# Turning the backward keys of a gated recurrence on VectorE, with DRAM in place of the full transpose

## The chip, the cores and the metric

The kernel runs on one core of a Trainium2 chip. Its engines run side by side, each through its own list of instructions in order: TensorE (PE in the profile; its weight loads are PEld), VectorE (DVE), ScalarE (ACT), GpSimd (POOL) and SyncE (SP), which issues nearly all DMA transfers. Semaphores hold an instruction until what it needs is there. The metric is the device time of one launch in microseconds (us), the median of several runs.

## The reference

One encoder block over 1024 tokens of width 1024: layer norm, one wide projection (11776 columns), a dilated window attention, a bidirectional gated recurrence, two gates, an output projection and a feed-forward part. The change lies in the recurrence. It has 8 heads with 128 key and 128 value channels, and is computed in chunks, once forwards and once backwards over the tokens:

```python
k_inv = k * jnp.exp(-cum)                       # cum: running log of the forget gate in a chunk
u = jnp.einsum('bhnck,bhncv->bhnkv', k * jnp.exp(cum_last - cum), v)
def step(state, inp):
    d, uu = inp
    return d[..., None] * state + uu, state
_, s_start = lax.scan(step, init, (decay, u))   # the state that each chunk starts from
o_inter = jnp.einsum('bhnck,bhnkv->bhncv', q_dec, s_start)
```

The product `u` sums over the tokens of a chunk. On TensorE the summed index must lie on the 128 partitions, for the keys as for the values.

## The kernel before, in words

All work is in 32-bit floats; the large projections are done as three products of split halves (`mm3`, lines 277 to 279, wide products of 128 x 512). The first phase runs these projections as one long stream of products (`stream`, 12 wide products per slot), four tiles of 128 columns at a time. Between the slots side work is fed in: the recurrence of head h as soon as its tiles are there, attention when its own are. This side work is a generator, and a number that it yields says how many slots pass before its next piece. So the list of pieces, with their yields, is the plan; a scheduler then orders the instructions of each engine by its own estimate of times, and what is written is the order in which each engine runs.

`hgrn_side` (line 1303) is the plan of one head. `hgrn_dir` prepares a direction in four steps: scans of the gates on VectorE (line 1189), then keys (`st["ki", d]`) by multiplications on GpSimd (lines 1197 and 1211), reciprocals (line 1208) and decayed queries (lines 1213 and 1216) on VectorE. Keys lie with the channel on the partition and the tokens of 8 chunks of 128 along the row. `hgrn_keys` (line 1219) turns them: eight 128 x 128 transposes on TensorE into two PSUM banks (line 1225), and two copies on ScalarE into tiles `hkT` of 128 x 512, one of a ring of five (`half`, line 791). `hgrn_states` (line 1230) multiplies seven turned chunks with the values (line 1240; four chunks from the first `hkT`, three from the second) and runs the states together on ScalarE and VectorE (lines 1242 and 1245). `hgrn_scores` (line 1249) and `hgrn_out` follow. The first direction's keys are turned after two steps of both directions, the second direction's right behind the first direction's states, three slots ahead of its own.

Nearly all transfers are issued by SyncE in one queue: weights (`wa`, line 256), stores of evacuated projections (`evh`, lines 578, 598, 609 and 628) and the fetches of the side work. An entry that waits, for its data or for its buffer, holds all that is queued behind it. Rows that are stored turned (`store_rows`, line 594) already go out in four transfers of 32 partitions x 16 runs of 32 floats.

Of the kernel before, what the change touches and what calls it, by code (L numbers as in the profile page):

```python
# [10 lines left out]
F32 = mybir.dt.float32  # L11
# [11 lines left out]
HALF = 512  # L23
# [56 lines left out]
class Block:  # L80
    evac_ahead = 1000

    def __init__(self, ctx, tc, x, ln_in_g, ln_in_b, w_in, hgrn_lb, hgrn_norm_g, w_att_up, w_hgrn_up,
                 w_o, ln1_g, ln1_b, w_ffn_in, w_ffn_out, ln2_g, ln2_b, tabs, out, dbg=None):
        self.tc, self.nc, self.ctx = tc, tc.nc, ctx
        self.x = x[0]
        self.ln = {"in": (ln_in_g, ln_in_b), "1": (ln1_g[0], ln1_b[0]), "2": (ln2_g[0], ln2_b[0])}
        self.w_in, self.lbw, self.ng = w_in[0], hgrn_lb, hgrn_norm_g[0]
        self.wa, self.wr, self.wo = w_att_up[0], w_hgrn_up[0], w_o[0]
        self.wfi, self.wfo, self.tabs, self.out = w_ffn_in[0], w_ffn_out[0], tabs, out[0]  # L90
        self.dbg = dbg or {}
        nc = self.nc

        self.npj = 0
        self.issued = {}
        self.psum = ctx.enter_context(tc.tile_pool(name="psum", bufs=1, space=PSUM))
        self.cst = ctx.enter_context(tc.tile_pool(name="cst", bufs=1))
        self.tiny = ctx.enter_context(tc.tile_pool(name="tiny", bufs=1))
        self.spare = self.pad(self.cst, CST_PAD)
        self.wpool = self.pool("wp", "right")  # L100
        self.wp = self.wpool.__enter__()
        dram = ctx.enter_context(tc.tile_pool(name="dram", bufs=1, space=DRAM))

        def scratch(name, n):
            if name in self.dbg:
                return [self.dbg[name][i] for i in range(n)]
            return [dram.tile([128, 1024], F32, name=f"{name}{i}") for i in range(n)]

        self.att_d = scratch("att", 4)
        self.rec_d = scratch("rec", 8)  # L110
        self.tg_d = scratch("tg", 16)
        self.n1_d = scratch("n1", 8)
        self.ahs_d = scratch("ahs", 8)
        self.hg_d = [{n: dram.tile([128, T], F32, name=f"hg{h}{n}") for n in ("t0", "t1", "q")}
                     for h in range(8)]
        self.at_d = [{(k, g): dram.tile([128, T], F32, name=f"at{j}{k}{g}") for k in "qk" for g in range(3)}
                     for j in range(4)]
        for h in range(8):
            self.hg_d[h].update({n: dram.tile([T, 128], F32, name=f"hg{h}{n}") for n in "vg"})
        for j in range(4):  # L120
            self.at_d[j].update({("v", g): dram.tile([T, 128], F32, name=f"at{j}v{g}") for g in range(3)})
        self.w_d = [dram.tile([32, 128], F32, name=f"wd{j}") for j in range(4)]
        self.td = [dram.tile([128, 4, HALF], F32, name=f"td{i}") for i in range(3)]
        self.gd = {p: dram.tile([128, NF // 2, HALF], F32, name=f"gd{p}") for p in range(1, 8)}
        self.consts()
# [1104 lines left out]
    def hgrn_states(self, st, d, kT, vT):  # L1230


        nc, dec = self.nc, st["dec", d]
        S = self.slot(6 + d, "hS", (8, 128))
        cs = list(range(8)) if d == 0 else list(range(7, -1, -1))
        for b in range(2):
# [4 lines left out]
            for jj, c, after in part:  # L1241
                nc.scalar.activation(S[:, after, :], ps[:, jj, :], AF.Copy, scale=dec[:, 2, c:c + 1])
            for _, c, after in part:
                if c != cs[0]:
                    nc.vector.scalar_tensor_tensor(S[:, after, :], S[:, c, :], dec[:, 2, c:c + 1], S[:, after, :],
                                                   op0=OP.mult, op1=OP.add)
        return S

# [23 lines left out]

    def hgrn_out(self, h, st, b, am, vT, S, sg):

        nc = self.nc
        po = self.ps_sd().rearrange("p (k c) -> p k c", k=4)
        for jj in range(4):
            c = 4 * b + jj
            terms = [(am[:, jj, :], vT[:, c, :])]
            if c > 0:  # L1280
                terms.append((st["qd", 0][:, c, :], S[0][:, c, :]))
            if c < 7:
                terms.append((st["qd", 1][:, c, :], S[1][:, c, :]))
            for n, (l, r) in enumerate(terms):
                nc.tensor.matmul(po[:, jj, :], l, r, start=(n == 0), stop=(n == len(terms) - 1))
        ss = self.smt.tile([128, 4], F32, name="hss", tag="hss", bufs=2)
        sq, on = self.half3("hsq"), self.half3("hon")
        nc.scalar.activation(sq, po, AF.Square)
        nc.vector.tensor_reduce(ss, sq, AX.X, OP.add)
        nc.gpsimd.tensor_scalar(ss, ss, 1.0 / 128, RMS_EPS, op0=OP.mult, op1=OP.add)  # L1290
        nc.gpsimd.tensor_tensor(ss, ss, self.mhalf[:, 0:4], OP.pow)
        g = sg[:, 4 * b:4 * b + 4, :]
        for jj in range(4):
            nc.vector.scalar_tensor_tensor(on[:, jj, :], po[:, jj, :], ss[:, jj:jj + 1], g[:, jj, :],
                                           op0=OP.mult, op1=OP.mult)
        r = g.rearrange("p k c -> p (k c)")
        nc.vector.transpose(r.rearrange("p (b k j) -> p k b j", b=4, k=4), on.rearrange("p k (b j) -> p k b j", j=32))
        dst = self.rec_d[h].rearrange("(b i) (h a x) -> a h i b x", b=4, h=2, a=4)
        for a in range(4):
            s = slice(32 * a, 32 * a + 32)  # L1300
            nc.sync.dma_start(dst[a, b], r[s, :].rearrange("i (b x) -> i b x", b=4))

    def hgrn_side(self, h, st):
        nc = self.nc
        vT = self.fetch_rows(5, "hv", self.hg_d[h]["v"])
        st["fa"] = self.slot(6, "fa")
        steps = [self.hgrn_dir(h, d, st) for d in range(2)]
        for _ in range(2):
            for z in steps:
                next(z)  # L1310
                yield 1
        k0 = self.hgrn_keys(st, 0)
        for z in steps:
            next(z)
        yield 2
        next(steps[0])
        yield 1
        S = {0: self.hgrn_states(st, 0, k0, vT)}
        k1 = self.hgrn_keys(st, 1)
        yield 2  # L1320
        next(steps[1])
        sg = self.fetch_rows(8, "hg", self.hg_d[h]["g"])
        yield 1
        S[1] = self.hgrn_states(st, 1, k1, vT)
        yield 3
        am = [self.hgrn_scores(st, b) for b in range(2)]
        yield -3
        for b in range(2):
            self.hgrn_out(h, st, b, am[b], vT, S, sg)
# [742 lines left out]
```

## Time and profile before

| what | value |
|---|---|
| median of 3 runs | 2017.85 us (2013.26 to 2018.37) |
| the profiled execution | 2016.71 us, its span 2014.9 us |
| PE / DVE / ACT / POOL busy | 98% / 68% / 45% / 50% of the span |
| granted TensorE clock, mean | 0.997 |
| mean share of the 16 DMA engines on SyncE's queue | 47.9% |
| issues on SyncE's queue in all | 1104 |

Rows of a timeline read: start and length in us, engine, line, operation, output<-inputs, shapes, count, and in brackets the idle time before it and what ended it. Rows of grouped instructions read: count, busy time in us, mean ns of one, idle time before. Rows of one line's instructions give the shortest, median and longest duration in ns; for transfers SPq is the issue on SyncE, and the landing is counted from the start of the issue. Heads are numbered 0 to 7 in the order in which they run; their recurrence lies between 100 and 960 us of the span.

### The profile page before, as it was taken

The page shows a single profiled execution, that of the slowest core. Times are in us where ns is not written, and L with a number is a line of the kernel's source. Part 1 is how long each engine was busy: PE and PEld are TensorE (multiplying, and loading weights), DVE is VectorE, ACT ScalarE, POOL GpSimd, SP SyncE. Part 2 cuts the span into 40 slices and gives each one's busy share as a digit, 9 for nine tenths or more (in the row PEclk, how much of TensorE's full clock was granted, in tenths as well). Part 3 has the DMA queues.
Part 4 walks back from the last instruction along what each step waited for, and adds up shares of the span by engine and source line. Part 5 has one row for each costly group of instructions (what it writes and reads, how often), then busy time and mean ns, then how long its engine had stood idle before and what let it go on. Part 6 is the DMA issues. An engine that isn't in the chain of part 4 may idle for free. (4 is left out here: it accounts for less than half of the span.)

```text
span 2014.9 us, 30820 instructions
## 1 busy us (share of the span) xinstructions
PE 1980.5 (98%) x10718; PEld 1640.8 (81%) x10718; DVE 1364.5 (68%) x2217; ACT 907.1 (45%) x1822; POOL 1006.3 (50%) x874
## 2 busy tenths in 40 slices
PE   7999999999999999999999999999999999999998
PEld 6688888888888888888888888888788888888886
DVE  7877746885467855797443236558777776767788
ACT  6554455543654446444464443345333333344541
POOL 6466643666455654565546562244666665620000
PEclk9999999999999999999999999999999999999999
DMA  5445645546455464555546377534434443447533
GB/s 162 126 121 151 164 131 149 140 119 173 108 158 141 132 156 118 152 147 151 141 122 190 121 252 245 156 121 141 140 127 136 145 137 125 144 166 276 167 103 123
DMA packets 416125, 301.17 MB, mean 149 GB/s; under 512 B 133153, under 2 KB 359394, under 8 KB 415970
## 3 DMA queue, kind: packets, MB, share of 16 engines
q1 hardware_dynamic: 410624, 282.14, 47.9%
q10 hardware_dynamic: 5346, 17.08, 2.2%
q8 instruction: 84, 1.38, 0.3%
q14 instruction: 71, 0.58, 0.1%
HBM read 204.96 MB, written 94.18 MB: 148 GB/s over the span
## 5 line engine op out<-in xcount | busy, mean ns | idle before, releaser
L229 POOL TENSOR_TENSOR w_lo<-wa,w_hi 128x512 fp32r<-128x512 f32 x272 | 366.3, 1355 | 230.5 <-ACT w_hi L219 216.6
L219 ACT CAST w_hi<-wa 128x512 fp32r<-128x512 f32 x272 | 168.2, 620 | 263.7 <-PE pj L278 166.2
L229 POOL TENSOR_TENSOR w_lo<-wsum,w_hi 128x512 fp32r<-128x512 f32 x88 | 127.8, 1462 | 111.1 <-PE sd L279 60.7
L229 POOL TENSOR_TENSOR w_lo<-f_raw,w_hi 128x512 fp32r<-128x512 f32 x66 | 101.2, 1540 | 51.5 <-ACT w_hi L219 50.3
L215 POOL TENSOR_TENSOR mv<-mv,mhalf 128x1 f32<-128x1 f32 x16 | 12.6, 790 | 221.7 <-DVE mv L214 221.6
L219 ACT CAST w_hi<-wsum 128x512 fp32r<-128x512 f32 x88 | 54.6, 621 | 116.7 <-PE sd L278 108.8
L277 PE MATMUL pj<-xt1hi,w_hi 128*128 128x512 f32 x252 | 99.0, 393 | 0.7 <-DVE evh L589 0.7
L219 ACT CAST gwsum<-a_raw 128x512 fp32r<-128x512 f32 (+1 forms) x78 | 48.1, 617 | 112.2 <-PE pj L278 56.0
L278 PE MATMUL pj<-xt1lo,w_hi 128*128 128x512 f32 x252 | 98.5, 391 | 0.0
L279 PE MATMUL pj<-xt1hi,w_lo 128*128 128x512 f32 x252 | 98.2, 390 | 0.0
L607 DVE TENSOR_TENSOR evh<-wkeep,pj 128x512 f32<-128x512 f32 x45 | 30.8, 685 | 99.4 <-PE pj L279 58.1
L727 POOL TENSOR_TENSOR wa<-wa,wa 128x512 f32<-128x512 f32 x46 | 65.8, 1431 | 57.1 <-DVE wa L726 56.2
L229 POOL TENSOR_TENSOR w_lo<-ws,w_hi 128x512 fp32r<-128x512 f32 x46 | 62.9, 1374 | 56.3 <-ACT w_hi L219 45.8
L755 ACT COPY wkeep<-pj 128x512 f32<-128x512 f32 x136 | 79.4, 585 | 4.9 <-DVE evh L577 4.7
L277 PE MATMUL pj<-xt2hi,w_hi 128*128 128x512 f32 x192 | 77.2, 403 | 2.0 <-ACT w_hi L219 2.0
L279 PE MATMUL pj<-xt2hi,w_lo 128*128 128x512 f32 x192 | 76.3, 397 | 2.0 <-POOL w_lo L229 2.0
L229 DVE TENSOR_TENSOR gwkeep<-a_raw,gwsum 128x512 fp32r<-128x512 f32 (+1 forms) x78 | 53.1, 681 | 36.1 <-ACT gwsum L219 33.3
L278 PE MATMUL pj<-xt2lo,w_hi 128*128 128x512 f32 x192 | 76.1, 396 | 0.8 <-DVE xt2lo L409 0.7
L277 PE MATMUL pj<-xt4hi,w_hi 128*128 128x512 f32 x192 | 76.2, 397 | 0.0
L278 PE MATMUL pj<-xb11lo,w_hi 128*128 128x512 f32 x192 | 75.3, 393 | 0.0
L278 PE MATMUL pj<-xt4lo,w_hi 128*128 128x512 f32 x192 | 75.2, 392 | 0.0
L277 PE MATMUL pj<-xb11hi,w_hi 128*128 128x512 f32 x192 | 75.0, 393 | 0.1
(438 smaller groups left out, 6481.7 us busy)
## 6 DMA issues: line engine op xcount, KB each, us to landing
wa<-in_w_in_dram SPq DMA_DIRECT2D x184, 256.0 KB, 3.4
f_raw<-in_w_ffn_in_dram SPq DMA_DIRECT2D x44, 512.0 KB, 4.2
a_raw<-gd SPq DMA_DIRECT2D x30, 512.0 KB, 3.6
gd<-fc SPq DMA_DIRECT2D x44, 256.0 KB, 2.0
gd<-fs SPq DMA_DIRECT2D x33, 256.0 KB, 2.5
tg<-evh SPq DMA_DIRECT2D x32, 256.0 KB, 3.4
tg<-tg SPq DMA_DIRECT2D x16, 512.0 KB, 5.9
y<-ahs SPq DMA_DIRECT2D x16, 512.0 KB, 6.6
```

The costliest lines, as they stand in the source:

```text
L215: nc.gpsimd.tensor_tensor(mv[:, 2:3], mv[:, 2:3], self.mhalf[:, 0:1], OP.pow)
L219: ins = nc.scalar.copy(hi, src) if eng_hi == "act" else nc.vector.tensor_copy(hi, src)
L229: ins = e.tensor_sub(lo, src, hi.bitcast(F32))
L277: nc.tensor.matmul(ps, whi, xhi, start=first, stop=False, **kw)
L278: nc.tensor.matmul(ps, whi, xlo, start=False, stop=False, **kw)
L279: self.product = nc.tensor.matmul(ps, wlo, xhi, start=False, stop=last, **kw).ins.name
L607: self.left(nc.vector.tensor_add(t, add, ps))
L727: nc.gpsimd.tensor_sub(a["a21"], a["a22"], a["a11"])
L755: nc.scalar.copy(t, ps)
```

## The change

Only the second (backward) direction is touched. Its keys are no longer transposed on TensorE. Right behind the first direction's transposes, VectorE turns each half of the keys (four chunks, 128 x 512) in blocks of 32 x 32, which leaves every block in its old place. The turned half is stored to a DRAM tile, and after two slots (second half: three) fetched back in four transfers, one for each group of 32 partitions, each of 32 x 16 runs of 32 floats, which puts the blocks where they belong. The states use the tiles as before; their piece of the plan stands where it stood.

```diff
+        self.kd = [[dram.tile([128, HALF], F32, name=f"kd{h}{n}") for n in range(2)] for h in range(8)]
...
         k0 = self.hgrn_keys(st, 0)
+        k1 = []
+        for b in (1, 0):
+            t = self.half("hkT")
+            nc.vector.transpose(t, st["ki", 1][:, 4 * b:4 * b + 4, :].rearrange("p k c -> p (k c)"))
+            nc.sync.dma_start(self.kd[h][b], t)
+            k1.append((t, self.kd[h][b].rearrange("(a i) (k b j) -> b i k a j", a=4, b=4, j=32)))
         for z in steps:
             next(z)
         yield 2
+
+        def back(t, z):
+            for b in range(4):
+                nc.sync.dma_start(t[32 * b:32 * b + 32, :].rearrange("i (k a j) -> i k a j", a=4, j=32), z[b])
+            return t.rearrange("p (k c) -> p k c", k=4)
+
+        k1[0] = back(*k1[0])
         next(steps[0])
         yield 1
+        k1[1] = back(*k1[1])
         S = {0: self.hgrn_states(st, 0, k0, vT)}
-        k1 = self.hgrn_keys(st, 1)
         yield 2
         next(steps[1])
         sg = self.fetch_rows(8, "hg", self.hg_d[h]["g"])
         yield 1
         S[1] = self.hgrn_states(st, 1, k1, vT)
```

The scheduler moves instructions too. Below are rows of the order on three engines; in the changed program all lines behind 121 are one higher up to `hgrn_side`, so that line 1241 there is line 1240 before, 278 is 277, and so on; 1317 is a turn on VectorE, 1318 the store, 1326 a load.

On PE, head 2, before: the first direction's states (7 products) and behind them the second direction's transposes.

```order
L279 MATMUL pj<-xb11hi,w_lo 128x512
L1240 MATMUL sd<-hv,hkT 128x128 x7
L1225 MATMUL sd<-tabs_sb,t_3587 128x128 x8
L277 MATMUL pj<-xb21hi,w_hi 128x512
L278 MATMUL pj<-xb21lo,w_hi 128x512
```

On PE, head 2, with the change: the second direction's states.

```order
L1241 MATMUL sd<-hv,hkT 128x128 x4
L278 MATMUL pj<-xt2hi,w_hi 128x512
L279 MATMUL pj<-xt2lo,w_hi 128x512
L280 MATMUL pj<-xt2hi,w_lo 128x512
L278 MATMUL pj<-xt1hi,w_hi 128x512
L1241 MATMUL sd<-hv,hkT 128x128 x3
L279 MATMUL pj<-xt1lo,w_hi 128x512
```

The transposes are gone, and these states, which stood together as seven, now stand as four and three with four wide products between.

On VectorE, head 2, with the change: the two turns between a reciprocal and the decayed queries, which followed each other before.

```order
L727 TENSOR_TENSOR wa_3496<-ws_3861,wa_3496 128x512
L1209 RECIPROCAL qd<-fb 128x4x64
L1317 STREAM_TRANSPOSE hkT<-t_3603 128x512 x2
L1214 SCALAR_TENSOR_TENSOR qd<-q,fa 128x8x64
L1217 SCALAR_TENSOR_TENSOR qd<-q,qd 128x8x64
```

On SyncE, head 7, before (`at3v`, `at3k`, `at3q`: stores and fetches for attention; `hg`: the gate's rows).

```order
L816 DMA hg<-hg7g 128x8x128
L806 DMA q_9899<-at3q_158 128x4x128 x2
L598 DMA at3v_190<-evh 32x16x32 x4
L578 DMA at3k_160<-evh 128x512
L256 DMA wa_9510<-in_w_in_dram 128x4x128
```

The same place with the change.

```order
L817 DMA hg<-hg7g 128x8x128
L1318 DMA kd_206<-hkT 128x512
L1318 DMA kd_205<-hkT 128x512
L807 DMA q_9915<-at3q_158 128x4x128 x2
L1326 DMA hkT<-kd_206 32x16x32 x4
L599 DMA at3v_190<-evh 32x16x32 x4
L579 DMA at3k_160<-evh 128x512
L1326 DMA hkT<-kd_205 32x16x32 x4
L257 DMA wa_9526<-in_w_in_dram 128x4x128
```

Both stores and the first half's loads stand in front of the stores of `at3v`, the second half's loads behind them.

## The prediction

> **What bounds the kernel now.** I read the page's busy shares first, then the list of PE's waits, then the timeline around the eight places where the second direction's keys are turned.
>
> ```profile
> span 2014.9 us, 30820 instructions
> PE 1980.5 (98%) x10718; PEld 1640.8 (81%) x10718; DVE 1364.5 (68%) x2217; ACT 907.1 (45%) x1822; POOL 1006.3 (50%) x874
> ```
>
> PE is busy for 98% of the span and takes its work in order. So an instruction taken off PE is worth the time it holds the next one back, and a new wait on PE costs its full length. VectorE, ScalarE and SyncE matter only through what PE waits for.
>
> In the profile's timeline of PE, head 6, this is what the removed piece costs (L1240: states of the first direction, each product shown as two rows; L1225: the eight transposes; L277 to L279: wide products):
>
> ```profile
> 856.52 1.72 PE L1240 MATMUL sd<-hv,hkT 128*128 128x128 f32 x14
> 858.08 1.04 PE L1225 MATMUL sd<-tabs_sb,t 128*128 128x128 f32 x8
> 858.87 0.48 PE L279 MATMUL pj<-xb22hi,w_lo 128*128 128x512 f32 x1
> 859.19 0.40 PE L277 MATMUL pj<-xb22hi,w_hi 128*128 128x512 f32 x1
> ...
> 864.45 0.39 PE L279 MATMUL pj<-xt4hi,w_lo 128*128 128x512 f32 x1
> ```
>
> Start to start is what counts, since products overlap: states and transposes together hold PE from 856.52 to 858.87, 2.35 us. From 859.19 to 864.45 stand 23 wide products: 0.228 us each. The first wide product after the narrow ones takes 0.32, so a change from narrow to wide costs 0.09. A block of states with no transposes behind it (head 3, second direction) takes 449.83 to 451.31, 1.48 us:
>
> ```profile
> 449.83 1.72 PE L1240 MATMUL sd<-hv,hkT 128*128 128x128 f32 x14
> 451.31 0.48 PE L277 MATMUL pj<-xb22hi,w_hi 128*128 128x512 f32 x1
> ...
> 440.70 1.09 PE L1225 MATMUL sd<-tabs_sb,t 128*128 128x128 f32 x8 [1.84 <-POOL t L1197]
> ...
> 684.41 1.10 PE L1225 MATMUL sd<-tabs_sb,t 128*128 128x128 f32 x8 [1.28 <-POOL t L1211]
> ...
> 924.54 1.09 PE L1225 MATMUL sd<-tabs_sb,t 128*128 128x128 f32 x8 [1.00 <-POOL t L1197]
> ```
>
> The brackets are the only long waits in front of these transposes: in heads 3, 5 and 7 PE reached them before GpSimd had finished the keys.
>
> **What is taken away.** Eight heads times (2.35 - 1.48) = 0.87 us: 7.0 us of PE. With the transposes go their three waits, 1.84 + 1.28 + 1.00 = 4.1 us; VectorE now waits for the keys instead, and comes late enough that only in heads 1 and 5 is anything left of it, 0.2 and 0.3 us (brackets further below). Sixteen copies leave ScalarE, which is 45% busy: nothing. Gain on PE: 11.1 us.
>
> **What is added on PE itself.** The order of the changed program splits the second direction's states into a group of four and a group of three, with wide products between: one more change from narrow to wide per head, 8 x 0.09 = 0.7 us.
>
> **What is added elsewhere: the way of the keys.** Per head two turns on VectorE, two stores and eight loads on SyncE's queue.
>
> ```profile
> L625 DVE STREAM_TRANSPOSE evh<-evh 128x512 f32<-128x512 f32 x14 | 9.6, 684 | 0.1
> ...
> at0v<-evh SPq DMA_DIRECT2D x24, 64.0 KB, 2.0
> at2k<-evh SPq DMA_DIRECT2D x6, 256.0 KB, 2.4
> ...
> L598 SPq DMA_DIRECT2D at0v<-evh x24: 303/488/786, 184.9 to 265.2; - x24
> ...
> L827 SPq DMA_DIRECT2D v<-at1v x8: 422/432/1498, 497.7 to 502.7; - x8
> ...
> DMA to landing us min/median/max: 2.4/4.1/6.2
> ```
>
> A turn of this shape takes 0.68 us. A 256 KB store of whole rows lands 2.4 us after its issue (2.0 is the 64 KB store in pieces of 32 x 16 x 32, the new loads' shape the other way round). Issues of that shape stand 0.49 us apart. The new load, 64 KB out of DRAM in 128-byte runs, is not in this trace. Its landing time R is bounded below by the 2.0 of the same pieces as a store and above by the 4.1 median of 64 KB loads with longer runs (last row: all of L827). I take the middle, 3.05: the direction is that of the loads, but the 4.1 comes from trains queued behind larger loads.
>
> So the first half of the keys is there 0.7 + 2.4 + 3 x 0.49 + 3.05 = 7.6 us after the turns begin, the second 4 x 0.49 later, at 9.6, if SyncE's queue holds nothing else (0.45 for each other transfer between).
>
> **When PE wants them.** For each head the timeline gives the start of the first direction's transposes (unchanged, PE row), and the VectorE instruction in front of which the turns now stand (its start is when they can begin):
>
> ```profile
> 130.73 1.03 PE L1225 MATMUL sd<-tabs_sb,t 128*128 128x128 f32 x8
> 139.99 0.68 DVE L1216 SCALAR_TENSOR_TENSOR qd<-q,qd 128x512 f32<-128x512 f32 x1
> 193.26 1.03 PE L1225 MATMUL sd<-tabs_sb,t 128*128 128x128 f32 x8
> 206.11 1.75 DVE L1213 SCALAR_TENSOR_TENSOR qd<-q,fa 128x512 f32<-128x512 f32 x1 [0.18 <-POOL t L1211]
> 366.43 1.03 PE L1225 MATMUL sd<-tabs_sb,t 128*128 128x128 f32 x8
> 377.15 1.59 DVE L1213 SCALAR_TENSOR_TENSOR qd<-q,fa 128x512 f32<-128x512 f32 x1
> 428.74 1.03 PE L1225 MATMUL sd<-tabs_sb,t 128*128 128x128 f32 x8
> 442.78 1.28 DVE L1245 SCALAR_TENSOR_TENSOR hS<-hS,dec 128x128 f32<-128x128 f32 x1
> 604.27 1.03 PE L1225 MATMUL sd<-tabs_sb,t 128*128 128x128 f32 x8
> 611.33 1.78 DVE L1213 SCALAR_TENSOR_TENSOR qd<-q,fa 128x512 f32<-128x512 f32 x1
> 666.61 1.03 PE L1225 MATMUL sd<-tabs_sb,t 128*128 128x128 f32 x8
> 684.39 1.75 DVE L1213 SCALAR_TENSOR_TENSOR qd<-q,fa 128x512 f32<-128x512 f32 x1 [0.34 <-POOL t L1211]
> 851.07 1.03 PE L1225 MATMUL sd<-tabs_sb,t 128*128 128x128 f32 x8
> 857.77 0.64 DVE L1216 SCALAR_TENSOR_TENSOR qd<-q,qd 128x512 f32<-128x512 f32 x1
> 905.22 1.03 PE L1225 MATMUL sd<-tabs_sb,t 128*128 128x128 f32 x8
> 926.64 0.63 DVE L1245 SCALAR_TENSOR_TENSOR hS<-hS,dec 128x128 f32<-128x128 f32 x1
> ```
>
> PE's arrival at the first group is start + 0.88 (transposes, change to wide) + n x 0.228 + 1.57 (first direction's states, change); n, counted in the changed program's order, is 65, 94, 67, 75, 69, 96, 54, 113 for heads 0 to 7. The second group comes 0.98 + m x 0.228 later, m = 4, 14, 4, 7, 6, 6, 7, 19. Head 3: 428.74 + 0.88 + 17.10 + 1.57 = 448.3, and the keys are there at 442.8 + 7.6 = 450.4: PE waits 2.1; its second group then comes at 453.0, keys 452.9, no wait. The same sum gives 0 in head 0 (148.0 against 147.6), 0.7 in head 2 and 1.1 in head 5.
>
> In the other four heads SyncE's queue decides, because a store in front of the loads waits for its own data:
>
> ```profile
> 217.28 1.96 SPq L598 DMA_DIRECT2D at0v<-evh  x4
> ...
> 614.36 2.97 SPq L598 DMA_DIRECT2D hg5g<-evh  x4
> ...
> 618.76 1.93 SPq L598 DMA_DIRECT2D hg5v<-evh  x4
> ...
> 857.87 1.96 SPq L598 DMA_DIRECT2D hg7v<-evh  x4
> ...
> 934.03 1.95 SPq L598 DMA_DIRECT2D at3v<-evh  x4
> ```
>
> These stores' data come from VectorE, now 1.4 us later behind the two turns. Head 7: the second half's loads stand behind at3v: 934.03 + 1.4 + 1.95 + 0.45 (one more store) = 937.8; the fourth load is issued at 939.3 and lands at 942.3, while PE, 0.9 late from the first half, comes at 939.6: 2.7 more, 3.6 in all. Head 4, behind hg5v and one store: the last load goes out at 623.6, lands at 626.6, PE comes at 624.8: 1.8. Head 1, behind at0v, which VectorE's new order serves some 2 us sooner: last load out at 219.6, landed 222.7, PE 221.3: 1.4. Head 6: hg7v holds the keys' stores until 859.8, 1.3 past the first turn: 0.9. Total of new waits: 0 + 1.4 + 0.7 + 2.1 + 1.8 + 1.1 + 0.9 + 3.6 = 11.6 us.
>
> **What else waits.** Behind a load that waits for its store's landing stand weight loads and evacuation stores on SyncE. I cost that at nothing, because weights are fetched a round of products ahead. VectorE's 16 x 0.68 = 10.9 us is covered too, except where scores follow it closely:
>
> ```profile
> PE sd L1262 <- DVE qd L1216: 0.4, 1, 0.4
> ```
>
> That is head 4; 1.4 us there and perhaps in head 6 is covered by PE's own new wait before the same scores. If that cover goes, 2.8 us.
>
> **Sum.** -7.0 - 4.1 + 0.7 + 11.6 = +1.2 us on the profiled execution, which took 2016.7 us with its 2014.9 us span: 2017.9. The median shown, 2017.85, is 1.1 above that execution. With R = 2.0 the new waits are 4.8 and the sum -5.6 (2011.1); with R = 4.1 they are 19.7, the sum +9.3 (2026.0).
>
> **The skill against the rows.** The rows have stores into DRAM landing after 2.0 (64 KB) and 2.4 us, 64 KB loads out of it after 4.1. The Trainium skill, DMA: Bandwidth & Descriptors, section Anatomy of one DMA, gives a fixed 2.0 us plus bytes over 436 GB/s, with the receipt heaviest when HBM is the target; an estimate by that page puts the load at 2.15 us, the store at 2.6 and the sum near -3.3, towards the quick-loads case below. The trace disagrees: here the loads are the slow direction. The same page's Specifications say pieces under 512 bytes miss the line rate; 128-byte stores at 2.0 us do not show it, and no row shows 128-byte loads. By that rule the slow-loads case is likelier, and I give it a little more than its symmetric share.
>
> **Rivals.**
> 1. *Quick loads* (R about 2.0): 2011.1. For it: same pieces, same queue, 2.0 us. Against: every load row is slower.
> 2. *PE never meets the loads*: the new waits stay near zero, because PE reaches the states later than my start-to-start sum says. All that is left is -11.1 + 0.7: 2006.3. For it: apart from head 3, PE is never over 1.1 us ahead of a first half. Against: between the two points this trace has PE waiting nowhere but at the three waits that go.
> 3. *Slow loads*, the case on the other side: eight short-run loads in a row on one in-order queue land like L827's, 4.1 us or later. 2026.0, and 2028.8 with the 2.8 of lost cover. It counts as slower from new waits of 17.6 us on (2023.9 - 2016.7 + 11.1 - 0.7), R = 3.8. Against: L827's trains follow larger loads.
>
> **Chances.** Between about 2011.8 and 2023.9, 0.3% either side of the median, this kernel's measurement can't tell a change. Forecast (R 2.4 to 3.8) 0.45; quick loads 0.14, half of it below the band; no waits 0.15; slow loads 0.26. With 0.03 of the forecast spilling over: faster 0.22, same 0.49, slower 0.29. The range runs from between rivals 1 and 2 to rival 3's end: 2008 to 2029.
>
> **What will show it.** PE's wait list should have states (L1240's line) waiting for DMA of hkT, about 10 us over about seven heads, longest in heads 7 and 3, and no waits at second-direction transposes. The landing times of hkT loads give R directly; under 2.4 or over 3.8 my size is wrong. If states wait little though R is near 3, the arrival sum is wrong; if long new waits stand at weights or scores, the cover is.

## The result and the profile after

The change is slower, by as much as this kernel's runs can just tell: 2020.51 us, median of 20 runs (2016.78 to 2027.51), beside 2014.36 us for the kernel before, median of 20 (2010.35 to 2021.89). The ratio is 1.0029 with a 95% interval of [1.0020, 1.0037], about 6 us. The profiled execution took 2024.13 us.

The head of the changed kernel's page:

```profile
span 2022.0 us, 30846 instructions
...
PE 1978.0 (98%) x10654; PEld 1633.6 (81%) x10654; DVE 1367.0 (68%) x2233; ACT 901.7 (45%) x1806; POOL 1009.2 (50%) x874
```

Its list of PE's waits, the rows for the states (us in total, times, longest):

```profile
PE sd L1241 <- DMA hkT<-kd: 13.8, 9, 2.5
...
PE sd L1241 <- DVE evh L578: 0.9, 1, 0.9
```

And head 0's first transposes in its timeline:

```profile
129.97 1.03 PE L1226 MATMUL sd<-tabs_sb,t 128*128 128x128 f32 x8
```

This place is a good mark, because what lies ahead of it varies by some 5 us from one execution to the next, whatever the kernel: in traces with 10.2 us or more at half the TensorE clock in the first 75 us, as in both of these, it stands at 130 to 132 us, in traces with 3.4 us of it or none at 125 to 128. From this mark to the end the change needs 2022.0 - 129.97 = 1892.0 us, the kernel before 2014.9 - 130.73 = 1884.2: 7.9 us more. The transposes are gone and so are PE's waits in front of the second direction's. In their place the states wait for the loads of their keys, 14.6 us in all (0.9 of it, in head 0, is put down to an evacuation; the landing of the last load in front of it is not in the trace, so that this too is a wait for the load is argued). PE's busy time fell by only 2.5 us, though 64 transposes worth 7.0 us went. That was the first sign that the wait list is not the whole story. The timeline of PE in head 3 shows why:

```profile
448.16 0.39 PE L280 MATMUL pj<-xb22hi,w_lo 128*128 128x512 f32 x1
450.91 2.04 PE L1241 MATMUL sd<-hv,hkT 128*128 128x128 f32 x8 [2.36 <-DMA hkT<-kd]
452.61 0.77 PE L278 MATMUL pj<-xb22hi,w_hi 128*128 128x512 f32 x1
453.18 0.63 PE L279 MATMUL pj<-xb22lo,w_hi 128*128 128x512 f32 x1
453.60 0.63 PE L280 MATMUL pj<-xb22hi,w_lo 128*128 128x512 f32 x1
454.03 0.52 PE L278 MATMUL pj<-xb22hi,w_hi 128*128 128x512 f32 x1
454.39 0.39 PE L279 MATMUL pj<-xb22lo,w_hi 128*128 128x512 f32 x1
454.62 0.39 PE L280 MATMUL pj<-xb22hi,w_lo 128*128 128x512 f32 x1
```

Behind the stall the four state products take 452.61 - 450.91 = 1.70 us, where the same group without a stall takes 0.8 (head 0), and the next three wide products start 0.42 to 0.57 us apart; from 454.39 on they are back at 0.23. Busy time in consecutive stretches of 3.41 us (columns: stretch and its length, busy us and instructions of PE, PEld, DVE, ACT, POOL, then the granted TensorE clock, the DMA share and GB/s):

```profile
447.48:450.89 3.41, 1.07 (x5) 0.57 (x4) 3.20 (x5) 0.20 (x1) 1.37 (x1) 1.00 0.58 93
450.89:454.30 3.41, 3.39 (x12) 3.12 (x13) 2.67 (x5) 1.14 (x4) 0.00 (x0) 0.50 0.64 150
...
624.96:628.38 3.42, 1.29 (x6) 0.74 (x4) 3.42 (x5) 0.26 (x1) 2.69 (x2) 1.00 0.62 139
628.38:631.79 3.41, 2.99 (x10) 2.73 (x11) 3.41 (x4) 2.20 (x8) 2.16 (x2) 0.50 0.29 42
935.58:938.99 3.41, 1.76 (x8) 1.13 (x6) 3.06 (x6) 0.30 (x2) 1.38 (x2) 1.00 0.86 189
938.99:942.41 3.42, 2.56 (x15) 2.32 (x16) 2.94 (x6) 1.89 (x6) 0.00 (x0) 1.00 0.45 68
```

After the stalls of head 3 and head 4 the granted clock is half for one such stretch: 2 x 3.41 x 0.5 = 3.4 us lost (3.2 if only PE's busy time in them, 3.39 and 2.99 us, is counted). After head 7's stall it is not. Waits and half clock make 18.0 us, and 18.0 + 0.7 - 11.1 = 7.6, against the 7.9 found.

The runs agree with it. Each run comes with its mean granted clock: 0.9961 over the 20 runs of the change, 0.9979 over 23 runs of the kernel before in a later round. The difference is worth 2018 x 0.0018 = 3.6 us of the 6. A run's mean also counts the half clock of its first 75 us, which differs between traces of the same kernel (10.2 and 3.4 us in two of the change), so the 3.6 is not shown to stand behind the states alone. But the kernels below in which no state waits for a load have 0.9970 to 0.9978, near the kernel before; those in which states wait have 0.9950 to 0.9959.

The steps of the way: the view of the turns (shortest, median and longest in ns), then of the stores and of the loads, each with its landing counted from the issue.

```profile
L1317 DVE STREAM_TRANSPOSE hkT<-t x16: 647/660/714, 139.2 to 930.0; 128x512 f32<-128x512 f32 x16
```

```profile
L1318 SPq DMA_DIRECT2D kd<-hkT x16: 319/344/1116, 140.0 to 930.7; - x16
...
DMA to landing us min/median/max: 2.0/2.2/4.7
```

```profile
L1326 SPq DMA_DIRECT2D hkT<-kd x64: 562/634/2240, 142.1 to 944.3; - x64
...
DMA to landing us min/median/max: 2.3/2.6/4.1
```

### The profile page after: what moved, and what is told of

It reads as the page before. It is cut to its first block, busy times and chain, and to the rows that moved or that the text cites. A ratio compares the mean times of both kernels' runs of the same rounds, so it can differ in the third digit from the quotient of the medians.

```text
span 2022.0 us, 30846 instructions
## 1 busy us (share of the span) xinstructions
PE 1978.0 (98%) x10654; PEld 1633.6 (81%) x10654; DVE 1367.0 (68%) x2233; ACT 901.7 (45%) x1806; POOL 1009.2 (50%) x874
## 5 line engine op out<-in xcount | busy, mean ns | idle before, releaser
L230 POOL TENSOR_TENSOR w_lo<-ws,w_hi 128x512 fp32r<-128x512 f32 x46 | 62.9, 1376 | 54.5 <-ACT w_hi L220 54.3
L280 PE MATMUL pj<-xt4hi,w_lo 128*128 128x512 f32 x192 | 75.0, 391 | 0.0
```

What stands on the lines that cost most here:

```text
L230: ins = e.tensor_sub(lo, src, hi.bitcast(F32))
L280: self.product = nc.tensor.matmul(ps, wlo, xhi, start=False, stop=last, **kw).ins.name
```

## The experiments

Theory A: the gain is real, and PE's waits for the loads, with the half clock behind some of them, eat it. Rivals: VectorE's turns cost something of themselves (B); the additional entries on SyncE's queue delay weights and evacuations (C). Each span below is counted from head 0's first transposes, as above: 1884.2 us before, 1892.0 with the change.

**The way beside the old one.** Turns, stores and loads are all done, and the states use keys from PE as before.

```diff
         k1[1] = back(*k1[1])
         S = {0: self.hgrn_states(st, 0, k0, vT)}
+        k1 = self.hgrn_keys(st, 1)
         yield 2
```

> The turns, stores and loads are done as in the change, but nothing uses them: the backward keys are transposed on PE and copied by ScalarE as before. Theory A: the trip costs nothing where PE doesn't wait for it; PE's order is the one before within 5 products, the three waits for GpSimd's keys stay: ratio 0.9995 to 1.001. Rival B or C (VectorE's 10.6 us, or 80 more entries on SyncE's queue and 1.1 us holds on it, delay evacuations and weights): ratio 1.003 or more, with new waits of PE for w_hi, w_lo, evh or DMA.

Measured: 1.0001 [0.9990, 1.0013]. The span on its page, the mark in its timeline, and three rows of PE's waits:

```profile
span 2016.2 us, 31011 instructions
```

```profile
130.60 1.03 PE L1226 MATMUL sd<-tabs_sb,t 128*128 128x128 f32 x8
```

```profile
PE sd L1226 <- POOL t L1198: 2.7, 2, 1.7
...
PE sd L1226 <- POOL t L1212: 1.2, 1, 1.2
...
PE sd L1263 <- DVE qd L1217: 1.1, 1, 1.1
```

1885.6 us, 1.4 above before; the three waits for GpSimd's keys are there as they were, and the one wait that VectorE lengthens is that of head 4's scores, by 0.7. So 10.6 us of turns and 80 transfers cost next to nothing where PE does not wait for their outcome. B and C fall.

**No trip.** The turns are made, nothing is stored or fetched, and the backward states use the forward keys.

```diff
-            nc.sync.dma_start(self.kd[h][b], t)
-            k1.append(...)
...
-        k1[0] = back(*k1[0])
...
-        k1[1] = back(*k1[1])
...
-        S[1] = self.hgrn_states(st, 1, k1, vT)
+        S[1] = self.hgrn_states(st, 1, k0[::-1], vT)
```

> Left out: stores and loads of the turned keys. VectorE makes both turns of every head as in the change, but nothing uses them; the backward states are computed from the forward keys in reversed order, so they need nothing new. PE's order is the one before without the backward transposes. Theory A (the gain is real, and PE's waits for the keys and the half clock behind two of them ate it): 9.5 to 11.5 us under the kernel before, ratio 0.9943 to 0.9955, no wait of the states, no half clock between 100 and 1000 us. Rival B (VectorE's 10.6 us of turns cost of themselves): 0.998 to 1.001, with waits of PE for VectorE or for evacuations.

Measured: 0.9942 [0.9930, 0.9954], 2002.44 us. Span and mark:

```profile
span 1999.9 us, 30676 instructions
```

```profile
125.77 1.03 PE L1226 MATMUL sd<-tabs_sb,t 128*128 128x128 f32 x8
```

1874.1 us: 10.1 less than before. No state waits, and there is no half clock between 100 and 1000 us. So the gain is real, with VectorE's turns in place: from the first transposes of head 0 to those of head 1 pass 61.66 us where before they were 62.53, from head 2's to head 3's 61.44 for 62.31, from head 6's to head 7's 53.31 for 54.15. That is 0.87, 0.87 and 0.84 for the transposes of one head. The change lies 17.9 above this kernel, near the 18.0 of its waits and its half clock; that sum leaves out the splits of the states (0.7) on the one side and on the other a wait of 1.5 for an attention maximum, which the change does not have.

**States two slots later.** The obvious remedy, if the loads come too late:

```diff
-        yield 1
+        yield 3
         S[1] = self.hgrn_states(st, 1, k1, vT)
-        yield 3
+        yield 1
         am = [self.hgrn_scores(st, b) for b in range(2)]
```

> The backward states are planned two slots later (24 wide products, 5.5 us), the scores stay where they were. In heads 0, 2, 3, 4 and 6 the states now stand as one group of seven, 7 to 18 products later for the last of them; in heads 1, 5 and 7 the order of PE is unchanged. Theory A: the waits of the five heads (0.9 + 0.6 + 2.4 + 2.5 + 1.3 = 7.7 us) and the half clock of heads 3 and 4 (3.3 us) go, some 7 us of waits in heads 1, 5 and 7 stay: 11 us under the change, 3 to 5 us under the kernel before, ratio 0.9975 to 0.9985. Rivals B and C (VectorE's turns or SyncE's longer queue cost, not the waits of the states): 1.002 to 1.004 as with the change.

Measured: 1.0029 [1.0015, 1.0044]: no gain over the change, and a miss. Three rows of PE's waits, then head 3 in the timeline:

```profile
PE sd L1241 <- DMA hkT<-kd: 10.7, 7, 2.4
...
PE sd L1286 <- POOL ham L1269: 1.4, 2, 0.7
...
PE sd L894 <- DVE M L835: 1.3, 1, 1.3
```

```profile
448.02 1.05 PE L1241 MATMUL sd<-hv,hkT 128*128 128x128 f32 x8
450.61 0.91 PE L1241 MATMUL sd<-hv,hkT 128*128 128x128 f32 x6 [1.53 <-DMA hkT<-kd]
```

In heads 0, 2, 4 and 6 the waits are gone, as expected. Head 3 still waits 1.53, because the group of seven now needs the second half where the group of four needed only the first. Heads 1, 5 and 7, whose order did not move, wait 9.2 instead of the 7 that I carried over. The half clock did not go either: it stands behind two other places, and over the runs the clock is 0.9959. Theory A's account (waits, half clock) holds for this kernel too, but that the waits of the other heads stay was wrong. In heads 1 and 5 VectorE begins the turns later here, 14.3 and 16.6 us after the head's first transposes where it was 12.7 and 15.1 in the change, and their waits grew by 1.3 each; in head 7 neither grew. What holds VectorE up there is open.

**Placing on the way out.** Four stores in short runs per half, one load of whole rows.

```diff
-            nc.sync.dma_start(self.kd[h][b], t)
+            z = self.kd[h][b].rearrange("(b i) (k a j) -> a i k b j", b=4, a=4, j=32)
+            for a in range(4):
+                nc.sync.dma_start(z[a], t[32 * a:32 * a + 32, :].rearrange("i (k b j) -> i k b j", b=4, j=32))
...
-            for b in range(4):
-                nc.sync.dma_start(t[32 * b:32 * b + 32, :]..., z[b])
+            nc.sync.dma_start(t, z)
```

> The blocks are placed on the way out (four stores of 32 partitions in 32-float runs per half) and come back in one transfer of whole rows. PE's order is that of the kernel without the trip; in five heads the first group of the states stands 8 products (1.8 us) later than in the change. Theory A: the states still wait, 5 to 9 us in all where the change has 14.7, since one load is issued in place of four; no stall over 2.3 us, so no half clock, except in the last head, where both loads stand behind the stores of at3v; ratio to the kernel before 0.997 to 0.9995. If a load of whole rows takes the 4.1 us of other 64 KB loads or more, waits of 10 to 14 us and ratio 1.000 to 1.002. Rival B (VectorE) and rival C (more entries on SyncE's queue hold weights up): 1.002 to 1.004 as with the change, and waits elsewhere than at the states.

(By the trace the first groups of the states stand 7 to 18 wide products later than in the change.) Measured: 1.0056 [1.0036, 1.0076]. The view of its stores (L1320 there), of its loads (L1327), and the row of PE's waits for them:

```profile
L1320 SPq DMA_DIRECT2D kd<-hkT x64: 573/627/1817, 135.0 to 934.4; - x64
```

```profile
L1327 SPq DMA_DIRECT2D hkT<-kd x16: 319/434/617, 140.7 to 941.5; - x16
...
DMA to landing us min/median/max: 2.9/3.7/5.8
```

```profile
PE sd L1241 <- DMA hkT<-kd: 18.0, 11, 2.9
```

The pieces cost 0.63 us of issue on either side. A load of whole rows, 256 KB, lands after 3.7 us where 64 KB in pieces took 2.6. The way got longer and the waits 18.0, against the 5 to 9 that I expected; the second case of the expectation (a landing of 4.1) was the nearer one, but its bounds were passed as well. No half clock stands in this trace between 100 and 1000 us, and its 1894.4 us are 20.3 above no trip: 18.0 of waits, 1.4 for one evacuation. The trace is of the fastest of six runs, with a clock of 0.999; the other five have 0.994 to 0.996 and will have had half clock, which no trace shows.

**ScalarE's queue.** Are the waits made by SyncE's queue, where loads stand behind stores that wait?

```diff
-            nc.sync.dma_start(self.kd[h][b], t)
+            nc.scalar.dma_start(self.kd[h][b], t)
...
-                nc.sync.dma_start(t[32 * b:32 * b + 32, :]..., z[b])
+                nc.scalar.dma_start(t[32 * b:32 * b + 32, :]..., z[b])
```

> The change with its stores and loads issued by ScalarE, in a queue of its own; PE's order is the change's within 13 products. Theory A2 (about half of the waits come from SyncE's queue, where the loads stand behind stores that wait for VectorE: head 1's second group, head 4's, both of head 7): from the turns' times, 2.2 us of store and 0.63 per load, the waits would be 0.5, 1.7, 0.2, 1.7, 0.3, 0, 0.8, 0.5 us for heads 0 to 7, 5.7 in all where the change has 14.7; no stall over 2 us, no half clock; 4 to 6 us under the kernel before, ratio 0.997 to 0.998. Theory A1 (the chain turn, store, load is too long in any queue): waits of 11 us or more, ratio 1.000 to 1.003. Rival D (ScalarE, in order and 45% busy, is held by the issues and by the wait for the store, and hands casts and copies over late): waits of PE for w_hi or evacuations of 6 us or more, ratio 1.000 or more.

Measured: 1.0051 [1.0037, 1.0065]. From PE's waits; from the view of the loads (who waited for them, and their landing); and stretches around head 5's second group:

```profile
PE sd L1241 <- DMA hkT<-kd: 9.1, 6, 2.9
...
PE sd L1241 <- issue: 4.5, 2, 3.4
```

```profile
  ACT evh L623: 5.7, 2
  POOL w_lo L230: 5.3, 2
  ACT w_hi L220: 4.8, 2
...
DMA to landing us min/median/max: 2.3/3.2/6.7
```

```profile
696.67:700.08 3.41, 0.68 (x3) 0.22 (x2) 1.89 (x4) 0.62 (x1) 2.08 (x2) 1.00 1.25 232
700.08:703.49 3.41, 2.77 (x24) 2.57 (x26) 0.60 (x2) 0.89 (x3) 0.00 (x0) 0.50 1.07 225
703.49:706.91 3.42, 3.42 (x59) 3.42 (x57) 1.51 (x4) 0.81 (x2) 0.74 (x2) 0.50 0.66 173
```

The states wait 14.4 in all, as with the change, but elsewhere: head 4 not at all, head 1 0.9 and head 7 2.8, whereas heads 3 and 5 wait 4.5 each. So SyncE's queue makes a part of the waits of heads 1, 4 and 7, but another queue does not save them: there ScalarE's own work is held, and the loads land later, 3.2 for 2.6 us. Half clock takes 8.5 us here. A2 falls as a way to gain, and A1 is left. Of D only the first half is seen, ScalarE held by the issues; PE's wait for `w_hi` is 2.0 us as in the change.

**Only where there is room.** Heads 0, 2, 4 and 6 by DRAM, with their states two slots later; heads 1, 3, 5 and 7 transposed by PE, one piece later in the plan.

```diff
+        k1, odd = [], h % 2
-        for b in (1, 0):
+        for b in () if odd else (1, 0):
...
         yield 2
+        if odd:
+            k1 = self.hgrn_keys(st, 1)
...
-        yield 1
+        yield 1 if odd else 3
         S[1] = self.hgrn_states(st, 1, k1, vT)
-        yield 3
+        yield 3 if odd else 1
```

> Heads 0, 2, 4 and 6 go by DRAM with their backward states planned two slots later, heads 1, 3, 5 and 7 are transposed on PE as before (in head 3 the transposes stand 24 products later, elsewhere where they stood). Theory A: in the even heads the last load lands 18 to 23 us after the first direction's transposes and PE comes at 21 to 24, so no wait over 0.5 us is left there; gain 4 x 0.87 for the transposes and 1.8 for head 3's wait: 4 to 6 us under the kernel before, ratio 0.997 to 0.998. Against it: the kernel with all states later had new waits elsewhere (0.7 twice for ham, 1.3 for an attention maximum with 1.7 of half clock behind it); if those come with the later plan itself: 0.9985 to 1.000.

Measured: 0.9991 [0.9979, 1.0003], 2011.90 us. Span, mark, and the idle time in the view of the states:

```profile
span 2007.5 us, 30820 instructions
```

```profile
126.22 1.03 PE L1226 MATMUL sd<-tabs_sb,t 128*128 128x128 f32 x8
```

```profile
its engine sat idle before it (us, times) until:
  PE sd L1241: 0.3, 1
```

1881.3 us, 2.9 below before; 4 to 6 were expected. The last rows are all the idle time in front of the states, and none of it is for DMA. But PE's waits for GpSimd's keys in front of the transposes that are left have shrunk, and not in head 3 alone:

```profile
PE sd L1226 <- POOL t L1212: 0.8, 2, 0.7
PE sd L1226 <- POOL t L1198: 0.3, 1, 0.3
```

These are 1.1 us in place of 4.1. Head 3's transposes, which stand 24 products later, no longer wait; those of heads 5 and 7 stand where they stood and wait 0 and 0.3 in place of 1.3 and 1.0. So 3.0 us of waits are gone, as much as the whole gain. The trace lets the two parts be told apart, since from one head's first transposes to the next head's PE has as many wide products as before. The four stretches that begin with head 0, 2, 4 and 6 take 62.8, 61.4, 62.9 and 54.4 us, before 62.5, 62.3, 62.3 and 54.2: 0.2 more in all. The four that begin with an odd head (the last ends with the span) are 3.1 shorter. So the way by DRAM brought nothing here that the trace shows, even with room, where 3.5 were expected. In the even heads PE now waits 2.5 us for scores, `ham` and an evacuation, before 0.4; the rest of the difference is open. A kernel in which only head 3's transposes are moved was not run. Timed again, because the interval reached over 1:

> The kernel with the way by DRAM in heads 0, 2, 4 and 6 only, timed again, since 0.9991 [0.9979, 1.0003] leaves open whether it is faster than the kernel before. By its trace it is: from head 0's first transposes to the end its span is 2.9 us shorter than before, no wait of states for DMA; expected ratio 0.998 to 0.9995. Against it: its mean granted clock in the first runs was 0.9970, before 0.9979, worth 1.8 us; if that is the kernel's own, the ratio is again 0.999 to 1.000.

Measured: 0.9978 [0.9967, 0.9989], 2009.92 us beside 2014.20, with mean clocks of 0.9978 and 0.9975, so the lower clock of the first runs was not the kernel's own. This version is faster than the kernel before in the second timing, and its ratio is below the change's in both. In the profile of this timing the span from the mark is 1883.5 us, 0.7 below before, with 3.41 us at half clock behind a wait of 1.1 for an attention maximum (L894); its even heads' stretches are 0.6 shorter than before, again not 3.5.

**The half clock.** Two more runs were made for it. In the first, PE was to be kept at work in the four longest stalls:

```diff
-        st["fa"] = self.slot(6, "fa")
+        st["fa"], st["h"] = self.slot(6, "fa"), h
...
+            if d == 1 and (st["h"], b) in ((3, 0), (4, 1), (7, 0), (7, 1)):
+                nc.tensor.matmul(ps, kT[b][0:32, 0, :], vT[0:32, 0:4, :], start=True, stop=True)
             for jj, c, _ in part:
                 nc.tensor.matmul(ps[:, jj, :], kT[b][:, c % 4, :], vT[:, c, :], start=True, stop=True)
```

> The change plus four products on PE whose result is not used: a 32x128 by 32x512 product from the first loaded quarter of the keys, in front of the states of head 3 (first half), head 4 (second half) and head 7 (both), where the change has stalls of 2.3 to 2.5 us. Each breaks its stall in two and runs inside it. Theory E (a PE that stands idle for over some 2 us is often given half the clock for the next 3.4 us, and this is part of the loss): waits of the states stay 12 to 15 us in all with none over 1.9 us, no half clock behind these four places, the granted clock over the runs goes from the change's mean of 0.9961 to 0.997 to 0.998 (before: 0.9979), and 2 to 3.6 us of the change's 6 come back: ratio to the kernel before 1.001 to 1.002. Theory F (the half clock has another cause and the stalls alone count): clock mean 0.996 as with the change, ratio 1.003 to 1.004.

Measured: 1.0048 [1.0032, 1.0065], mean clock 0.995. The stalls were not broken; from PE's waits:

```profile
PE sd L1243 <- DMA hkT<-kd: 8.0, 7, 1.7
PE sd L1241 <- DMA hkT<-kd: 5.7, 2, 3.7
```

The added products (L1241 here) waited themselves, 2.0 us in head 3 and 3.7 in head 7, since the first quarter came hardly sooner than the last. So the run tells nothing between E and F by its time. Its 3.7 us in head 7 are the longest stall of all these traces behind the first 75 us, and 6.8 us of half clock follow; 6.8 follow head 3's 2.0 too, and 3.4 follow head 4's 1.7. The second is the change once more:

> The changed kernel itself, a second profile. If the half clock depends on where a stall falls in some running count: the same ten stalls within 0.3 us, 14 to 15 us in all, but half clock behind other stalls of over 2 us than those of heads 3 and 4, or behind more or fewer of them. If it belongs to the place: again heads 3 and 4, and not head 7.

Measured: 2022.24 us; from PE's waits:

```profile
PE sd L1241 <- DMA hkT<-kd: 12.5, 9, 2.7
...
PE sd L1241 <- DVE evh L578: 1.5, 1, 1.5
PE sd L1241 <- DVE qd L1217: 1.3, 1, 1.3
```

15.3 us of waits, in the same heads but for head 1, which has none this time; single stalls differ by up to 1.7, more than the 0.3 that I expected. Half clock follows head 4's stall (2.65) alone. Head 3's (2.10) and head 7's (2.58) go without, so it doesn't belong to the place. What the traces show of it stands in the last section.

## Why the prediction came out as it did

The time predicted was 2017.9 in 2008 to 2029; 2020.51 lies in it. The shift predicted was +1.2 us, and measured are 6 (4.0 to 7.5, by the ratio's interval). That the time came out closer than the shift is luck: the execution that the shift was added to, 2016.7, lay 2.3 above the median of twenty of the kernel before, 2014.36. "Within 0.3%" was the likeliest case, and 1.0029 stands on its edge.

- **Gain, 11.1 us: right.** No trip is 10.1 to 11.7 faster (by span and by ratio), with 0.84 to 0.87 for one head's transposes where 0.87 was taken.
- **Splits, 0.7:** not measured apart; the account closes to within 0.3 us with it.
- **VectorE and the rest of SyncE's queue at nothing: right**, by the way beside the old one (1.4 us by span, 1.0001 by ratio).
- **The length of the way: right by two errors that cancel.** The load's landing R was taken as 3.05 and is 2.6; the store's 2.4 is 2.2; an issue of a load was taken as 0.49 and is 0.63. By these medians the first half takes 0.66 + 2.2 + 3 x 0.63 + 2.6 = 7.4 (predicted 7.6), the second 4 x 0.63 = 2.5 more, 9.9 (9.6), with nothing else on the queue. In the trace they took 7.4 to 11.0 and 9.8 to 16.9, as far as landings are recorded. R lies between the quick case and mine, well below the 3.8 at which slow loads were to decide. Why the 64 KB loads of the trace before took 4.1 was not looked into further. The estimate by the Trainium skill's page DMA: Bandwidth & Descriptors, section Anatomy of one DMA, had the store (2.6) slower than the load (2.15); the rows have 2.2 and 2.6, so here again the load is the slower one. That section's figures are for transfers that GpSimd issues, and these go through SyncE's queue, so it was no measure for them.
- **New waits, 11.6 us: mechanism right, the term 3.0 too small.** It measured 14.6. By heads:

| head | 0 | 1 | 2 | 3 | 4 | 5 | 6 | 7 | sum |
|---|---|---|---|---|---|---|---|---|---|
| predicted | 0 | 1.4 | 0.7 | 2.1 | 1.8 | 1.1 | 0.9 | 3.6 | 11.6 |
| measured | 0.9 | 1.7 | 0.4 | 2.4 | 2.5 | 0.7 | 1.3 | 4.8 | 14.6 |

  The places are those predicted, and head 0; head 7 comes first as predicted, then heads 4 and 3. Head 7 has the largest part of the excess, 1.2, and it is in the store: it landed after 4.7 us (the row's maximum), not 2.4, so the first group waited 2.5 instead of 0.9. Why a store takes twice as long there is not settled; it took 4.7 to 4.8 at this place with states two slots later and on ScalarE's queue too. A 512 KB fetch of the gate's rows was issued half a us ahead of it each time.
- **The step that failed** is the sentence "a new wait on PE costs its full length". It can cost more: two of the ten stalls were followed by 3.41 us at half clock. This added up to 3.4 us in the profile, and the mean clock over the runs is lower by as much (3.6). The prediction had no term for it. Nothing in the trace of before pointed to it between 100 and 1000 us, where no stall is over 1.84 us; the kernel's start has such stretches at 49 and 62 us, which I had not looked into.
- **Sum:** +1.2 + 3.0 + 3.4 = 7.6, the trace +7.9.

Of the rivals, quick loads and no waits at all are ruled out by R and by the wait list. Of the three, slow loads (2026.0) came nearest in time, but not by its mechanism.

## What to carry to other kernels

When the bound engine runs at 98%, a transfer on its path has to land with room to spare in every one of its places: here the way cost nothing when nobody waited for it (1.0001), and ate more than its gain when PE did. Count a stall of over some 2 us on TensorE at its length and half of 3.4 us more, at times half of 6.8. Room alone does not make a gain: with the move only in the four heads with room nobody waited for a load, and yet by the trace those heads ran no faster, because other waits took the place. When a mixed version is faster (0.1 to 0.2% here), look at which of its parts did it: here it was the odd heads, whose waits for GpSimd's keys had gone.

## What the runs showed of the hardware

**Half clock after stalls of some 2 us.** In eleven traces of these kernels all stretches of half clock last 3.41 us or twice that, apart from the one at the end of each span, and within a trace they start on one grid of 3.41 us that runs on, stalls or not (450.89 and 628.38 above lie 52.0 steps apart). I laid that grid over each trace from 75 to 1990 us and took PE's idle time in each step. All 8 steps with 2.03 us of idle time or more (of 3.41) were followed by half clock; of 27 steps with 1.2 to 1.91 us, 3 were, and of all the others one, with 1.1 us. Two of these four lie at the wait for the attention's maximum (L894, quoted above); what sets them apart is open. The kernel's start, from 20 to 75 us, is not in these counts and is less clear: 11 of its 15 steps with 1.55 to 1.96 us of idle time were followed by half clock, and one with 1.82 was not. So the idle time of a step is not all that decides. It fits that the same stall does or does not cost more: head 7's 2.51 us fell across two steps, 1.65 in the first (1.76 busy in the rows above) and 0.86 in the second, and head 3's 2.36 almost wholly into one. In the second profile of the change head 4's stall put 2.32 into one step, and heads 3 and 7, without half clock, 1.81 and 1.91. The kernel that places on the way out waits longest of all, 18.0 us, but never over 1.82 in one step, and its trace has no half clock there. That a stall was the cause was not shown by breaking it, since the attempt with added products failed; it rests on these counts, and on the kernels in which no state waits for a load, whose traces have no half clock from 75 to 1990 us, apart from the one at L894 in the second trace of the mixed version. The Trainium skill, page TensorE: Matmul & The Clock Gate, section What's actually happening, describes a free-running window of 3413 ns and half rate after an idle window. The traces agree with the window and the rate; they differ in that 2.03 us of idle time in a window were enough.

**Loads in pieces and in rows.** A 64 KB load out of DRAM in 128-byte runs landed after 2.6 us and its issue held SyncE for 0.63; the 256 KB load of whole rows took 0.43 to issue and 3.7 to land. Stores of the keys in such runs took 0.63 to issue too, but line 598's stores of 32 x 16 x 32 took 0.49 in the trace before; what makes the difference is open.
